# A transformer trunk with 2-D attention and an RWKV-7 scan: attention heads issued in pairs, scan features without half-height products and without Pool's products

## The chip, the cores and the metric

The kernel runs on one core of a Trainium2 chip. The core has a matrix engine (TensorE: PE, and PEld for its weight loads), a vector engine (DVE), a scalar engine (ACT), Pool (GpSimd) and a sync engine (SP) that mostly issues DMAs; each works through its own instructions in order and waits on semaphores for the others. Matrix products write PSUM, which DVE and ACT copy out. The metric is device time in microseconds of one execution; less is better.

## The reference

Two layers over 1024 latent tokens (a grid of 16 rows by 64 columns) and 256 context tokens, width 1024, float32. Layer 0 mixes with window pooling and neighbourhood attention, layer 1 with RWKV-7 in both directions; each layer ends with a squared-ReLU MLP. The two parts that the change touches:

```python
def neighbourhood_attention(q, k, v, k_ctx, v_ctx, rpb):
    ...
        s_lat = jnp.einsum('bqhd,brkhd->bhqrk', q_row, k_band).astype(jnp.float32) * scale
        ...
        s_lat = jnp.where(col_ok[:, None, :], s_lat + bias, NEG_INF)
        s_ctx = jnp.einsum('bqhd,bchd->bhqc', q_row, k_ctx).astype(jnp.float32) * scale
        s = jnp.concatenate([s_lat.reshape(B, NA_HEADS, GRID_W, kr * GRID_W), s_ctx], axis=-1)
        p = jax.nn.softmax(s, axis=-1).astype(v.dtype)
        ...
def rwkv_features(h, mu, ...):
    ...
    v = heads(xv @ wv)
    kk = heads(k * k_k)
    kk = kk * lax.rsqrt(jnp.maximum(jnp.sum(kk * kk, axis=-1, keepdims=True), 1e-24))
    ...
    for d in range(2):
        w_raw = heads(w0[d] + jnp.tanh(xw @ w1[d]) @ w2[d])
        decay = jnp.exp(-jnp.exp(-jax.nn.softplus(-w_raw) - 0.5))
        a = jax.nn.sigmoid(heads(a0[d] + (xa @ a1[d]) @ a2[d]))
        k_d = kh * (1 + (a - 1) * k_a_h)
```

## The kernel before

Stages follow each other on one core: layer 0's mixer (`l0_mixer`: norms, values, then the attention from 158 to about 575 us, then its output products), the MLP, the projections of layer 1 (`l1_features`), the scan features (`l1_scan_features`, about 1941 to 2299 us), the scan over chunks of 64 tokens (`l1_scan`), its readout, the last MLP. Large products split each float32 operand into a high and a low part (`split`: ACT casts the high part, DVE subtracts) and take three products (`mm3`); small ones are plain float32, and PE runs two instructions for each.

*Attention.* A unit is one head and one block of 128 queries: 8 heads in four pairs `hp` with member `hh`, 8 latent blocks (`rb`, `cb`) and 2 context blocks each, 80 units, the two heads of a pair one after the other. The two heads of a pair lie in the two halves of the 128 partitions (`half[hh]`). A unit's `scores` (L714) multiplies q and k over the head's 64 features: `sc`, 128 queries by 256 context keys, and for latent blocks `sl`, by 384 neighbouring keys. DVE adds the bias and finds the maximum, ACT takes the exponential with the sum. `normalise` (L743) divides on DVE. `transposed` (L749) turns five blocks of 128 keys on PE in groups of three and two (tile `ptps`), ACT and DVE copy them out. `outputs` (L766) multiplies by the values into 64 of the 128 partitions of `o`. The order is written out by hand: turn i issues scores of unit i, a fill, the transposes of unit i - 1, a fill, the outputs of unit i - 2, a fill, the normalising of unit i. A `fill` (L682) takes 1.17 steps of a generator `bg`, each one round of three products: first the projections of later heads and of the pooling (tile `acc`), then, when enough heads are done (`FIRST_OUT`, counted in units), the mixer's output products. What the fills haven't issued follows after the loop. PSUM: two buffers for `sl`, one for `sc`, two for `ptps`.

*Scan features.* A unit is 256 tokens by one pair of heads: 8 units of context tokens, then 32 of latent ones. In turn u:

- `decays(u+2)` multiplies the two lora inputs `xa` (decay and a, two directions d) by `w2h` over 128 rows (64 features twice: the inputs' high part in one half, their low part in the other) and by `w2l` over the 64 rows of the high part (tile `pw`, 8 products); ACT takes tanh of them (`sg`, `th`).
- `exps(u+1)` takes ACT's two exponentials of the running sums (`pe`, `cum`) and the key factor `kd`, which Pool multiplies by k.
- `scaled(u)` makes the four scaled features `F` on DVE; Pool copies the chunk ends to `pcs` and forms the bonus sums `ks`; SP writes `F` to DRAM.
- `scores(u-1)` takes the products `lp`, `bonuses(u-2)` multiplies `ks` (`bp`), `norms(u+2)` spreads the key norms by a product of 64 rows (`kn`, from `rn` and `sel`), `sums(u+2)` scans `sg` on DVE.
- Between them stand the value products (24 `acc` products over 128 rows, their transposes `vtr`). `value_lo` makes the low part `wl` of the next value weights, on Pool, once in four units. Steps of the first inversion (`tmp`, `X` on DVE) run along the latent units.

The scan's `chain_s` multiplies its state by a column of `pcs`.

Of the kernel before, what the change touches and what calls it, by code (L numbers as in the profile page):

```python
# [10 lines left out]
F32 = mybir.dt.float32  # L11
# [8 lines left out]
D = 1024  # L20
# [23 lines left out]
FIRST_OUT = 67  # L44
# [13 lines left out]
class Trunk:  # L58
# [240 lines left out]
    def l0_mixer(self):  # L299
# [143 lines left out]
        scp = self.pool(es, "scps", 1, PSUM)  # L443
        ptp = self.pool(es, "ptps", 2, PSUM)
# [106 lines left out]
        def out_products():  # L551
# [94 lines left out]
            for t in range(NT):  # L646
                ready = (FIRST_OUT, FIRST_OUT + 8, FIRST_OUT + 12)[(t + 1) // 4 if t + 1 < NT else 2]
# [53 lines left out]

        units = []
        for hp in range(4):
            units += [(hp, rb, cb, hh) for rb in range(2) for cb in range(4) for hh in range(2)]
            units += [(hp, None, t, hh) for t in range(2) for hh in range(2)]
        U = [dict() for _ in units]

        def bias_load(i):
            hp, rb, cb, hh = units[i]
            if rb is not None:  # L710
                b = U[i]["bias"] = atp.tile([128, 384], F32, tag="bias", name="bias", bufs=6)
                nc.sync.dma_start(out=b, in_=a["bias"][hp * 2 + hh, :, rb, CB_TYPE[cb]])

        def scores(i):  # L714
            hp, rb, cb, hh = units[i]
            w = U[i]
            q, k = qk[0, hp][half[hh]], qk[1, hp][half[hh]]
            if rb is None:
                q = q[:, L + cb * 128:L + (cb + 1) * 128]
            else:  # L720
                q = q[:, 0:L].rearrange("p (rb cb i) -> p rb cb i", rb=2, cb=4)[:, rb, cb]
            nl = 0 if rb is None else 384
            n = w["n"] = nl + 256
            sc = scp.tile([128, 256], F32, tag="sc", name="sc")
            nc.tensor.matmul(out=sc, lhsT=q, rhs=k[:, L:T], start=True, stop=True)
            p = w["p"] = atp.tile([128, 640], F32, tag="p", name="p", bufs=3)
            m = w["m"] = atp.tile([128, 8], F32, tag="m", name="m", bufs=3)
            nc.vector.tensor_tensor_reduce(
                out=p[:, nl:n], in0=sc, in1=zeros.to_broadcast([128, 256]), scale=1.0, scalar=-3.0e38, op0=ALU.add, op1=ALU.max, accum_out=m[:, 0:1]
            )  # L730
            top = m[:, 0:1]
            if nl:
                sl = slp.tile([128, 384], F32, tag="sl", name="sl")
                k3 = k[:, 0:L].rearrange("p (r c) -> p r c", c=GW)[:, 4 * rb:4 * rb + 12, C0[cb]:C0[cb] + 32]
                nc.tensor.matmul(out=sl, lhsT=q, rhs=k3, start=True, stop=True)
                nc.vector.tensor_tensor_reduce(
                    out=p[:, 0:nl], in0=sl, in1=w["bias"], scale=1.0, scalar=top, op0=ALU.add, op1=ALU.max, accum_out=m[:, 1:2]
                )
                top = m[:, 1:2]
            nc.vector.tensor_scalar(out=m[:, 2:3], in0=top, scalar1=-1.0, scalar2=None, op0=ALU.mult)  # L740
            nc.scalar.activation(out=p[:, 0:n], in_=p[:, 0:n], func=AF.Exp, bias=m[:, 2:3], accum_out=m[:, 4:5])  # L741

        def normalise(i):  # L743
            w = U[i]
            p, m, n = w["p"], w["m"], w["n"]
            nc.vector.reciprocal(out=m[:, 5:6], in_=m[:, 4:5])
            nc.vector.tensor_scalar(out=p[:, :n], in0=p[:, :n], scalar1=m[:, 5:6], scalar2=None, op0=ALU.mult)

        def transposed(i):  # L749
# [1450 lines left out]
```

## Time and profile before

| | us |
|---|---|
| median of 3 runs | 3671.38 (3670.8 to 3674.52) |
| profiled execution | 3669.7, its span 3667.9 |
| window 158 to 575 (attention) | 417 |
| window 1941 to 2299 (scan features) | 358 |

The profile is of one execution. PE's busy time is modelled, since matmuls overlap: the start of one to the start of the next says more than its duration. A group's row reads: line, engine, operation, output from inputs, shapes, count, then busy us and mean ns of one, then idle us before it and what ended that. In PE rows 64\*128 stands for 64 rows of the array by 128 columns. A row of a line's own view has minimum/median/maximum ns and the first and last start.

### The profile page before, as it was taken

The numbers are of one execution on the slowest core, as the hardware profiler recorded it, in microseconds if no ns is written. First come the engines' busy times: TensorE is split into PE (matmuls) and PEld (weight loads), VectorE is DVE, ScalarE is ACT, GpSimd is POOL, SyncE is SP. The second block draws the span as 40 slices with busy tenths as digits, with TensorE's granted clock in tenths as the row PEclk, the third lists the DMA queues.
The fourth block names the chain that finished last, engine by engine and source line by source line (L and its number), as shares of the span: only waits on it lengthen the run. The fifth ranks groups of instructions, "written<-read, shape, count | busy, mean of one in ns | idle before, by whom it ended". The sixth has DMA issues, their size and how long they took to land. (4 is left out here: it accounts for less than half of the span.)

```text
span 3667.9 us, 61460 instructions
## 1 busy us (share of the span) xinstructions
PE 3472.9 (95%) x25002; PEld 2833.8 (77%) x25002; DVE 2100.3 (57%) x3796; ACT 1445.7 (39%) x2659; POOL 583.4 (16%) x761
## 2 busy tenths in 40 slices
PE   8999999999999999999999998788988899999998
PEld 4777767788888888977887776677877688888887
DVE  4144555534444444477757989688755834444446
ACT  5223335522121211247767555656655441112122
POOL 0010020010101000004433555222231300000000
PEclk9999999999999999999998988799999999999999
DMA  8412224322222220133225666989885331111112
GB/s 278 139 58 69 62 91 132 130 84 80 92 70 92 69 74 31 58 111 94 82 79 156 202 213 207 207 179 196 186 200 146 130 101 46 46 46 47 52 52 75
DMA packets 434027, 409.05 MB, mean 112 GB/s; under 512 B 152992, under 2 KB 363808, under 8 KB 433744
## 3 DMA queue, kind: packets, MB, share of 16 engines
q1 hardware_dynamic: 405376, 321.55, 30.1%
q0 software_dynamic: 24032, 81.81, 8.1%
q8 instruction: 197, 3.23, 0.4%
q10 hardware_dynamic: 4336, 1.77, 0.2%
q14 instruction: 86, 0.70, 0.1%
HBM read 292.54 MB, written 112.49 MB: 110 GB/s over the span
## 5 line engine op out<-in xcount | busy, mean ns | idle before, releaser
L896 DVE TENSOR_TENSOR yacc<-yps,yacc 128x512 f32<-128x512 f32 x540 | 369.9, 690 | 304.1 <-PE yps L92 303.6
L73 ACT CAST wh<-st 128x1024 fp32r<-128x1024 f32 x160 | 165.1, 1048 | 758.2 <-PE yps L92 557.8
L92 PE MATMUL yps<-wh,xh 128*128 128x512 f32 x1152 | 453.2, 393 | 4.3 <-DVE yacc L896 2.6
L92 PE MATMUL yps<-wh,xl 128*128 128x512 f32 x1152 | 448.5, 390 | 1.4 <-DVE xl L74 1.4
L92 PE MATMUL yps<-wl,xh 128*128 128x512 f32 x1152 | 448.9, 390 | 0.0
L74 DVE TENSOR_TENSOR wl<-st,wh 128x1024 fp32r<-128x1024 f32 x160 | 194.4, 1229 | 264.8 <-ACT wh L73 262.6
L92 PE MATMUL acc<-h2h,wh 128*128 128x426 f32 (+3 forms) x768 | 274.4, 357 | 3.0 <-ACT y L670 3.0
L92 PE MATMUL acc<-h2h,wl 128*128 128x426 f32 (+3 forms) x768 | 273.2, 356 | 0.0
L92 PE MATMUL acc<-h2l,wh 128*128 128x426 f32 (+3 forms) x768 | 272.9, 355 | 0.0
L92 PEld LDWEIGHTS yps<-wh,xh 128*128 128x128 f32 x1152 | 216.2, 188 | 72.2 <-DVE yacc L896 13.2
L92 PEld LDWEIGHTS yps<-wh,xl 128*128 128x128 f32 x1152 | 216.2, 188 | 48.4 <-DVE xl L74 3.0
L92 PEld LDWEIGHTS yps<-wl,xh 128*128 128x128 f32 x1152 | 216.4, 188 | 44.9 <-issue 1.7
L878 DVE TENSOR_TENSOR r<-r 128x428 f32<-128x428 f32 (+4 forms) x164 | 102.4, 625 | 240.5 <-ACT r L877 240.5
L92 PE MATMUL acc<-mh,wh 128*128 128x256 f32 (+1 forms) x640 | 223.1, 350 | 4.3 <-ACT mh L73 4.2
L92 PE MATMUL acc<-ml,wh 128*128 128x256 f32 (+1 forms) x640 | 214.4, 335 | 0.0
L92 PE MATMUL acc<-mh,wl 128*128 128x256 f32 (+1 forms) x640 | 214.0, 335 | 0.0
L92 PE MATMUL acc<-h2bh,wh 128*128 128x512 f32 (+3 forms) x544 | 211.4, 389 | 1.4 <-ACT wh L73 0.7
L92 PE MATMUL acc<-h2bl,wh 128*128 128x512 f32 (+3 forms) x544 | 211.1, 388 | 0.8 <-DVE h2bl L287 0.7
L92 PE MATMUL acc<-h2bh,wl 128*128 128x512 f32 (+3 forms) x544 | 210.9, 388 | 0.3 <-DVE wl L74 0.3
L877 ACT ACTIVATE r<-acc 128x428 f32<-128x428 f32 (+4 forms) x164 | 89.1, 543 | 291.5 <-PE acc L92 272.5
L741 ACT ACTIVATE p<-p,m 128x640 f32<-128x640 f32 (+1 forms) x80 | 61.3, 766 | 260.2 <-DVE m L740 256.8
L92 PEld LDWEIGHTS acc<-h2h,wh 128*128 128x128 f32 x768 | 144.2, 188 | 15.9 <-issue 5.1
(324 smaller groups left out, 7520.7 us busy)
## 6 DMA issues: line engine op xcount, KB each, us to landing
st<-in_mlp_w SPq DMA_DIRECT2D x128, 512.0 KB
ft<-F SPq DMA_DIRECT2D x64, 512.0 KB
adas<-in_ada_w POOLq DMA_DIRECT2D x112, 256.0 KB, 3.8
adas<-in_ada_w SPq DMA_DIRECT2D x80, 256.0 KB
BK<-ft POOLq DMA_DIRECT2D x38, 512.0 KB, 6.9
AR<-ft POOLq DMA_DIRECT2D x64, 256.0 KB, 8.0
x<-x SPq DMA_DIRECT2D x28, 512.0 KB
bias<-in_bias SPq DMA_DIRECT2D x64, 192.0 KB
```

The costliest lines, as they stand in the source:

```text
L73: self.nc.scalar.copy(out=hi, in_=src)
L74: self.nc.vector.tensor_tensor(out=lo, in0=src, in1=hi.bitcast(F32), op=ALU.subtract)
L92: self.nc.tensor.matmul(out=ps, lhsT=lhs[x], rhs=rhs[y], start=first and i == 0, stop=last and i == 2)
L741: nc.scalar.activation(out=p[:, 0:n], in_=p[:, 0:n], func=AF.Exp, bias=m[:, 2:3], accum_out=m[:, 4:5])
L877: nc.scalar.activation(out=r, in_=ps, func=AF.Relu)
L878: nc.vector.tensor_tensor(out=r, in0=r, in1=r, op=ALU.mult)
L896: nc.vector.tensor_tensor(out=yacc[t][:, n], in0=ps, in1=yacc[t][:, n], op=ALU.add)
```

## The change

**Attention.** A unit is now a pair of heads, 40 units in all. `scores` issues the two heads' `sc` next to each other, then the two `sl`; DVE and ACT follow with both heads. `outputs` takes the two heads by turns for each block of keys. `transposed` treats the ten blocks of a pair (four in a context unit) in groups of four, four and two, called with a part number between the three fills. The outputs of unit i - 2 now stand right behind the scores of unit i. `sc` gets a second PSUM buffer, `ptps` loses one; `fill` takes 2.34 steps, and `FIRST_OUT` and the clocks count in pairs.

**Scan features.** `w2l`, `sel` and `rn` are 128 rows high, so the products `pw` and `kn` run over all rows; `w2l` then also meets the low part of its inputs. Pool's products (`kd`, `ks`, `value_lo`, half of the split of `w2l`) are made by DVE, and its copies to `pcs` by one copy on ACT; Pool keeps a small memset. `pcs` is laid out by pair and time block, and `chain_s` indexes it so. ACT's tanh is issued after `scaled` (`gates`), ACT's key factor behind it (`keys`); `bonuses` follows one unit behind. `v`, `ls`, `kd` and `ks` have one buffer in place of two, `th` two in place of three.

```diff
-FIRST_OUT = 67
+FIRST_OUT = 33
+FILL = 2.34
...
-        scp = self.pool(es, "scps", 1, PSUM)
-        ptp = self.pool(es, "ptps", 2, PSUM)
+        scp = self.pool(es, "scps", 2, PSUM)
+        ptp = self.pool(es, "ptps", 1, PSUM)
...
-            for _ in range(int(turn[0] * 1.17) - int((turn[0] - 1) * 1.17)):
+            for _ in range(int(turn[0] * FILL) - int((turn[0] - 1) * FILL)):
...
+            sc = [scp.tile([128, 256], F32, tag="sc", name="sc") for _ in two]
+            for hh in two:
+                nc.tensor.matmul(out=sc[hh], lhsT=qs[hh], rhs=ks[hh][:, L:T], start=True, stop=True)
             if nl:
-                sl = slp.tile([128, 384], F32, tag="sl", name="sl")
-                k3 = k[:, 0:L].rearrange("p (r c) -> p r c", c=GW)[:, 4 * rb:4 * rb + 12, C0[cb]:C0[cb] + 32]
-                nc.tensor.matmul(out=sl, lhsT=q, rhs=k3, start=True, stop=True)
...
+        def transposed(i, part):
+
             w = U[i]
-            p, n = w["p"], w["n"]
-            pt = w["pt"] = atp.tile([128, 640], F32, tag="pt", name="pt", bufs=2)
-            done = 0
-            for cnt in ((3, 2) if n == 640 else (2,)):
-                ps = ptp.tile([128, 384], F32, tag="pt", name="ptps")
-                for j in range(cnt):
-                    nc.tensor.transpose(
-                        out=ps[:, j * 128:(j + 1) * 128], in_=p[:, (done + j) * 128:(done + j + 1) * 128], identity=self.ident
-                    )
-                dst = pt[:, done * 128:(done + cnt) * 128]
-                if cnt == 3:
-                    nc.scalar.copy(out=dst, in_=ps[:, :cnt * 128])
-                else:
-                    nc.vector.tensor_copy(out=dst, in_=ps[:, :cnt * 128])
-                done += cnt
+            nb = w["n"] // 128
+            if part == 0:
+                w["pt"] = atp.tile([128, 2 * nb, 128], F32, tag="pt", name="pt", bufs=2)
+            blocks = [(hh, j) for hh in two for j in range(nb)][4 * part:4 * part + 4]
+            if not blocks:
+                return
+            ps = ptp.tile([128, 4, 128], F32, tag="pt", name="ptps")[:, :len(blocks)]
+            for b, (hh, j) in enumerate(blocks):
+                nc.tensor.transpose(out=ps[:, b], in_=w["p"][hh][:, j * 128:(j + 1) * 128], identity=self.ident)
+            dst = w["pt"][:, 4 * part:4 * part + len(blocks)]
+            if part == 1:
+                nc.vector.tensor_copy(out=dst, in_=ps)
+            else:
+                nc.scalar.copy(out=dst, in_=ps)
...
             for j, v in enumerate(vs):
-                nc.tensor.matmul(
-                    out=op[half[hh], cb], lhsT=v, rhs=w["pt"][:, j * 128:(j + 1) * 128], start=j == 0, stop=j == len(vs) - 1
-                )
+                for hh in two:
+                    nc.tensor.matmul(
+                        out=op[half[hh], cb], lhsT=v[:, half[hh]], rhs=w["pt"][:, hh * nb + j], start=j == 0, stop=j == nb - 1
+                    )
...
+                clock[0] = 2 * i
+                if i + 2 < nu:
+                    bias_load(i + 2)
+                if i % 10 == 2 and i < 30:
+                    heads(i // 10 + 1)
                 if i < nu:
                     scores(i)
+                if i > 1:
+                    outputs(i - 2)
                 fill()
                 if 0 < i <= nu:
-                    transposed(i - 1)
+                    transposed(i - 1, 0)
+                settle(2 * i)
                 fill()
-                if i > 1:
-                    outputs(i - 2)
-                settle(i)
+                if 0 < i <= nu:
+                    transposed(i - 1, 1)
+                clock[0] = 2 * i + 1
+                settle(2 * i + 1)
                 fill()
+                if 0 < i <= nu:
+                    transposed(i - 1, 2)
                 if i < nu:
                     normalise(i)
             settle()
...
-            wl = cp.tile([128, 2, D], F32R, name="w2l")
+            wl = cp.tile([128, 4, D], F32R, name="w2l")
             for i in range(4):
                 fr = slice(i * 256, i * 256 + 256)
                 wst = self.wst.tile([128, 4, 256], F32, tag="st", name="w2")
                 nc.sync.dma_start(out=wst, in_=a["w2s"][:, :, fr])
-                nc.scalar.copy(out=wh[:, :, fr], in_=wst)
-                for d in range(2):
-                    h = half[d]
-                    (nc.gpsimd if d else nc.vector).tensor_tensor(
-                        out=wl[h, :, fr], in0=wst[h, d::2], in1=wh[h, d::2, fr].bitcast(F32), op=ALU.subtract
-                    )
+                self.split(wh[:, :, fr], wl[:, :, fr], wst)
...
-        sel = cp.tile([64, 8, 128], F32R, name="sel")
+        sel = cp.tile([128, 8, 128], F32R, name="sel")
...
-            self.rn = bigp.tile([64, T], F32R, name="rn")
+            self.rn = bigp.tile([128, T], F32R, name="rn")
...
-                nc.gpsimd.tensor_tensor(out=vw[m + 1][1], in0=vst[0], in1=vw[m + 1][0].bitcast(F32), op=ALU.subtract)
+                nc.vector.tensor_tensor(out=vw[m + 1][1], in0=vst[0], in1=vw[m + 1][0].bitcast(F32), op=ALU.subtract)
...
-                    nc.tensor.matmul(out=ps[:, i], lhsT=wl[half[d], i, fr], rhs=x[half[d]], start=False, stop=True)
+                    nc.tensor.matmul(out=ps[:, i], lhsT=wl[:, 2 * i + d, fr], rhs=x, start=False, stop=True)
...
-            for d in range(2):
-                nc.gpsimd.tensor_tensor(out=kd[:, d], in0=kd[:, d], in1=rv(w["x"][:, 0], d), op=ALU.mult)
...
+            for d in range(2):
+                nc.vector.tensor_tensor(out=kd[:, d], in0=kd[:, d], in1=rv(w["x"][:, 0], d), op=ALU.mult)
...
+            nc.scalar.copy(out=self.pcs[:, hp, t0 // 256], in_=pe[:, :, CH])
...
-                nc.gpsimd.tensor_copy(out=self.pcs[:, d, hp, sl], in_=pe[:, cs, CH])
...
-                ks = w["ks"] = tp.tile([128, n], F32, tag="ks", name="ks", bufs=2)
-                nc.gpsimd.tensor_tensor(out=ks, in0=kd[:, 0], in1=rv(kd[:, 1], 1), op=ALU.add)
-                nc.gpsimd.tensor_tensor(out=ks, in0=ks, in1=rt, op=ALU.mult)
+                ks = w["ks"] = tp.tile([128, n], F32, tag="ks", name="ks", bufs=1)
+                nc.vector.tensor_tensor(out=ks, in0=kd[:, 0], in1=rv(kd[:, 1], 1), op=ALU.add)
+                nc.vector.tensor_tensor(out=ks, in0=ks, in1=rt, op=ALU.mult)
...
+                if u + 2 < nu:
+                    gates(u + 2)
+                if u + 1 < nu:
+                    keys(u + 1)
                 if u % 8 == 5 and u + 3 < nu:
                     self.xan = activations(self.xt)
                 if u + 3 < nu:
...
                     value_out(v - 1)
                 if u:
                     scores(u - 1)
-                if u >= 2:
-                    bonuses(u - 2)
+                    bonuses(u - 1)
...
-            for u in range(nu - 1, nu):
-                bonuses(u)
...
+                c = chunk_of(s, d)
+                pc = (c // 4) * 8 + d * 4 + (3 - c % 4 if d else c % 4)
                 nc.vector.tensor_tensor(
-                    out=SS[d], in0=src, in1=self.pcs[:, d, :, s:s + 1].to_broadcast([128, 8, CH]), op=ALU.mult
+                    out=SS[d], in0=src, in1=self.pcs[:, :, pc // 8, pc % 8:pc % 8 + 1].to_broadcast([128, 8, CH]), op=ALU.mult
                 )
```

PE near the end of the attention, where few products of other work stand between (`sc`, `sl` scores; `ptps` transposes; `o` outputs; `acc` a pooling product). Before, one unit and the next:

```order
L725 MATMUL sc<-kT,qT 128x256
L735 MATMUL sl<-kT,qT 128x384
L757 MATMUL ptps<-ident,p 128x128 x5
L781 MATMUL o<-pt,vlat 64x128 x3
L781 MATMUL o<-pt,vctx 64x128 x2
L496 MATMUL acc<-pd,poolw 128x426
L725 MATMUL sc<-kT,qT 128x256
```

And of the change, one pair:

```order
L731 MATMUL sc<-kT,qT 128x256 x2
L736 MATMUL sl<-kT,qT 128x384 x2
L795 MATMUL o<-pt,vlat 64x128 x6
L795 MATMUL o<-pt,vctx 64x128 x4
L772 MATMUL ptps<-ident,p 128x128 x4
L497 MATMUL acc<-pd,poolw 128x426
L772 MATMUL ptps<-ident,p 128x128 x4
L497 MATMUL acc<-pd,poolw 128x426
L772 MATMUL ptps<-ident,p 128x128 x2
```

Both heads' scores now stand together, the outputs come straight after them, and the transposes are parted by the fills.

DVE in one latent unit of the scan features (`th`, `F`: scaled features; `xa`: the next inputs' low part, only in one unit of eight; `cum`: the scan). Before:

```order
L1333 SCALAR_TENSOR_TENSOR th<-th,kk 128x256 x2
L1336 TENSOR_TENSOR F<-th,cum 128x8x64
L1340 TENSOR_TENSOR F<-kk,pe 128x4x64
L1342 TENSOR_TENSOR F<-kd,cum 128x4x64
L1347 TENSOR_TENSOR F<-k,pe 128x4x64
L1340 TENSOR_TENSOR F<-kk,pe 128x4x64
L1342 TENSOR_TENSOR F<-kd,cum 128x4x64
L1347 TENSOR_TENSOR F<-k,pe 128x4x64
L1206 TENSOR_TENSOR xa<-xt,xa 64x512 x2
L1305 SCALAR_TENSOR_TENSOR cum<-smask,sg 128x512
```

And of the change:

```order
L1357 SCALAR_TENSOR_TENSOR th<-th,kk 128x256 x2
L1360 TENSOR_TENSOR F<-th,cum 128x8x64
L1364 TENSOR_TENSOR F<-kk,pe 128x4x64 x2
L1366 TENSOR_TENSOR kd<-kd,k 128x256 x2
L1370 TENSOR_TENSOR F<-kd,cum 128x4x64
L1375 TENSOR_TENSOR F<-k,pe 128x4x64
L1370 TENSOR_TENSOR F<-kd,cum 128x4x64
L1375 TENSOR_TENSOR F<-k,pe 128x4x64
L1388 TENSOR_TENSOR ks<-kd 128x256
L1389 TENSOR_TENSOR ks<-ks,k 128x256
L1221 TENSOR_TENSOR xa<-xt,xa 64x512 x2
L1327 SCALAR_TENSOR_TENSOR cum<-smask,sg 128x512
```

DVE's own rows stay, and Pool's four products of 256 columns stand among them.

More of the change, by code (lines that the diff above doesn't have):

```diff
@@ new lines, in scores @@
+            if nl:
+                sl = [slp.tile([128, 384], F32, tag="sl", name="sl") for _ in two]
+                for hh in two:
+                    k3 = ks[hh][:, 0:L].rearrange("p (r c) -> p r c", c=GW)[:, 4 * rb:4 * rb + 12, C0[cb]:C0[cb] + 32]
+                    nc.tensor.matmul(out=sl[hh], lhsT=qs[hh], rhs=k3, start=True, stop=True)
+            w["p"] = [atp.tile([128, 640], F32, tag="p", name="p", bufs=4) for _ in two]
+            w["m"] = [atp.tile([128, 8], F32, tag="m", name="m", bufs=4) for _ in two]
@@ L736, in scores @@
+            for p, m, s in zip(w["p"], w["m"], sc):
                 nc.vector.tensor_tensor_reduce(
[L737 removed]
+                    out=p[:, nl:n], in0=s, in1=zeros.to_broadcast([128, 256]), scale=1.0, scalar=-3.0e38, op0=ALU.add, op1=ALU.max, accum_out=m[:, 0:1]
                 )
[L739 to L740 removed]
@@ L741, in scores @@
-            nc.scalar.activation(out=p[:, 0:n], in_=p[:, 0:n], func=AF.Exp, bias=m[:, 2:3], accum_out=m[:, 4:5])
+            for hh in two:
+                p, m = w["p"][hh], w["m"][hh]
+                top = m[:, 0:1]
+                if nl:
+                    nc.vector.tensor_tensor_reduce(
+                        out=p[:, 0:nl], in0=sl[hh], in1=w["bias"][hh], scale=1.0, scalar=top, op0=ALU.add, op1=ALU.max, accum_out=m[:, 1:2]
+                    )
+                    top = m[:, 1:2]
+                nc.vector.tensor_scalar(out=m[:, 2:3], in0=top, scalar1=-1.0, scalar2=None, op0=ALU.mult)
+                nc.scalar.activation(out=p[:, 0:n], in_=p[:, 0:n], func=AF.Exp, bias=m[:, 2:3], accum_out=m[:, 4:5])
@@ L767, in outputs @@
         def outputs(i):
-            hp, rb, cb, hh = units[i]
+            hp, rb, cb = units[i]
             w = U[i]
             vlat, vctx = att[hp]
-            first, last = (cb, hh) == (0, 0), (cb, hh) == ((1, 1) if rb is None else (3, 1))
+            first, last = cb == 0, cb == (1 if rb is None else 3)
             if first:
@@ L776, in outputs @@
             op, cat = att["o"], att["cat"]
-            vs = [vctx[:, j, half[hh]] for j in range(2)]
+            nb = w["n"] // 128
+            vs = [vctx[:, j] for j in two]
             if rb is not None:
-                vs = [vlat[:, cb * 4 + rb + j, half[hh]] for j in range(3)] + vs
+                vs = [vlat[:, cb * 4 + rb + j] for j in range(3)] + vs
             for j, v in enumerate(vs):
-                nc.tensor.matmul(
-                    out=op[half[hh], cb], lhsT=v, rhs=w["pt"][:, j * 128:(j + 1) * 128], start=j == 0, stop=j == len(vs) - 1
-                )
+                for hh in two:
+                    nc.tensor.matmul(
+                        out=op[half[hh], cb], lhsT=v[:, half[hh]], rhs=w["pt"][:, hh * nb + j], start=j == 0, stop=j == nb - 1
+                    )
             if last:
@@ L799, in l0_mixer @@
         heads(0)
-        for i in range(4):
+        for i in range(2):
             bias_load(i)
```

71 lines of the change are left out of this document (36 added, 35 removed).

## The prediction, made before the changed kernel was run

> **What bounds the kernel now.** I read the page's busy shares first, then the windows of the two stages that the change touches, then the PE timeline inside each, and last the groups of DVE.
>
> ```profile
> PE 3472.9 (95%) x25002; PEld 2833.8 (77%) x25002; DVE 2100.3 (57%) x3796; ACT 1445.7 (39%) x2659; POOL 583.4 (16%) x761
> ```
>
> PE is busy for 95% of the span, so what counts is how long PE's own stream is, stage by stage. The windows below are the attention (158 to 575 us), the context units of the scan features (1941 to 2010) and their latent units (2010 to 2299). Columns: length, then busy PE, PEld, DVE, ACT, POOL, granted clock, DMA share.
>
> ```profile
> 158.00:575.00 417.00, 406.71 (x2109) 290.31 (x2110) 213.44 (x667) 132.86 (x291) 40.15 (x25) 0.99 0.26 78
> 1941.00:2010.00 69.00, 69.00 (x527) 52.75 (x527) 51.02 (x84) 52.09 (x108) 25.20 (x45) 0.88 0.53 162
> 2010.00:2299.00 289.00, 258.02 (x2222) 209.72 (x2223) 266.93 (x489) 165.04 (x346) 159.08 (x239) 0.88 0.69 209
> ```
>
> The attention is bound by PE (406.7 of 417 us, DVE at half). The context units are too (69.0 of 69.0). The latent units are not: there DVE has 267 of 289 us and PE 258. So a saving on PE counts in full in the first two windows, and hardly in the third; there only DVE's sum counts.
>
> **The change, part by part: attention.** One head's turn on PE, with the fill products (`acc`, three per round) between:
>
> ```profile
> 301.41 0.70 PE L725 MATMUL sc<-kT,qT 64*128 64x256 f32 x2
> 301.95 0.80 PE L735 MATMUL sl<-kT,qT 64*128 64x384 f32 x2
> 302.68 0.47 PE L92 MATMUL acc<-h1h,wh 128*128 128x428 f32 x1
> 302.99 0.36 PE L92 MATMUL acc<-h1l,wh 128*128 128x428 f32 x1
> 303.18 0.36 PE L92 MATMUL acc<-h1h,wl 128*128 128x428 f32 x1
> 303.38 0.71 PE L757 MATMUL ptps<-ident,p 128*128 128x128 f32 x5
> 303.84 0.44 PE L92 MATMUL acc<-h1h,wh 128*128 128x428 f32 x1
> 304.12 0.36 PE L92 MATMUL acc<-h1l,wh 128*128 128x428 f32 x1
> 304.31 0.35 PE L92 MATMUL acc<-h1h,wl 128*128 128x428 f32 x1
> 304.59 0.87 PE L781 MATMUL o<-pt,vlat 128*64 128x128 f32 x6
> 305.30 0.60 PE L781 MATMUL o<-pt,vctx 128*64 128x128 f32 x4
> 305.83 0.46 PE L92 MATMUL acc<-h1h,wh 128*128 128x428 f32 x1
> ```
>
> Durations overlap, so I take differences of starts. Scores use 64 of 128 rows (64*128) and take 302.68 - 301.41 = 1.27 us; outputs use 64 of 128 columns (128*64) and take 305.83 - 304.59 = 1.24; five transposes take 0.46. A fill product normally steps by 0.19 (302.99 to 303.18), but by 0.31 right after the scores, 0.28 right after the transposes and 0.28 ahead of the outputs: each change of the array's shape costs some 0.1 us. A head has five such places (into and out of scores, into and out of outputs, out of the transposes), 0.5 us. A pair of heads thus costs 2 x (1.27 + 1.24 + 0.46 + 0.5) = 6.94 us beside its fill.
>
> What two heads cost when issued side by side in the two halves isn't shown in this stage, but the scan shows it:
>
> ```profile
> 2398.00 1.04 PE L1581 MATMUL sa<-AR,BK 128*64 128x128 f32 x16
> 2509.30 2.05 PE L1596 MATMUL sr<-AR,BK 128*128 128x128 f32 x16
> ```
>
> Both rows are 16 instructions over 128 columns; `sa` writes the two column halves by turns, `sr` uses the whole array. `sa` takes 1.04 us, `sr` 2.05: neighbours in different halves run at the same time. For outputs this is the very form (128*64, halves by turns), so a pair costs about 1.24 in place of 2.48. For row halves the nearest row is `lp` (quarters on the diagonal, rows and columns both different):
>
> ```profile
> 2099.78 1.15 PE L1370 MATMUL lp<-F 64*64 64x64 f32 x32
> 2100.86 0.61 PE L1385 MATMUL bp<-rkbd,ks 128*128 128x2 f32 x4
> 2101.40 0.38 PE L1298 MATMUL kn<-rn,sel 64*128 64x256 f32 x1
> 2101.71 0.38 PE L92 MATMUL acc<-mh,wh 128*128 128x256 f32 x1
> 2101.93 0.28 PE L92 MATMUL acc<-ml,wh 128*128 128x256 f32 x1
> 2102.05 0.28 PE L92 MATMUL acc<-mh,wl 128*128 128x256 f32 x1
> ...
> 2103.24 0.28 PE L1285 MATMUL pw<-xa,w2h 128*128 128x256 f32 x1
> 2103.45 0.38 PE L1286 MATMUL pw<-xa,w2l 64*128 64x256 f32 x1
> ...
> 2105.64 0.39 PE L92 MATMUL acc<-mh,wh 128*128 128x256 f32 x1
> ```
>
> 32 instructions of 64 columns in 1.08 us (2100.86 - 2099.78) are 2048 columns, as many as `sr`'s 16 of 128 in 2.05: again about half. So bounds for a pair's scores are 1.27 (full overlap) and 2.54 (none); I take 1.27, both overlapping rows being near a half. The Trainium skill ("TensorE: Matmul & The Clock Gate", Measured speedup vs the span model) gives four row tiles a speedup of 3.07, not 4. Two tiles at that efficiency would gain 1.54, and by an estimate from that page the attention would save about 13 us less than I say. No run here shows row halves alone.
>
> After the change a pair costs 1.27 + 1.24 + 0.92 for ten transposes, plus five places of 0.1 (into scores, out of outputs, out of three groups of transposes; scores and outputs now stand next to each other): 3.93 us. It saves 3.0 us for each of the 32 latent pairs. The 8 context pairs have 256 of 640 score columns (0.54 from 301.41 to 301.95) and 4 of 10 output products (0.53 from 305.30 to 305.83), so they save 0.54 + 0.53 + 0.5 = 1.6. Sum 32 x 3.0 + 8 x 1.6 = 109 us. Fill work is the same: 2.34 rounds for a pair against 1.17 for a head, thresholds halved.
>
> Costed at nothing: the second transpose buffer goes, so each group of four blocks must be copied out before the next. Between groups stands a fill of two or three rounds (2 x 0.58 = 1.2 us), which covers a copy of 512 columns (under 0.83, the exponential of 640 columns, quoted below). Near the end, where fills have no products left, the cover is gone and a copy costs up to 0.8 us three times for some five pairs. I take 4 us for that, so **attention -105**. After it DVE would have 213 of 312 us, 68%: still no bound.
>
> **Scan features, PE.** A 64-row product between 128-row ones costs 0.3 us in place of 0.12 (2101.93 to 2102.05): the eight `pw` products take 2105.64 - 2103.24 = 2.40 us, and over 128 rows 8 x 0.12 = 0.96. `kn` falls from 0.31 to 0.12 and its follower from 0.22 to 0.12. Together 1.7 us a unit. Over the nine units in the context window this is 15 us of 69, but ACT (52 us, plus small copies of `pcs`) and DVE (51, plus two products a unit for `kd`) are close behind. Bounds 3 and 15; I take 10.
>
> **Scan features, DVE.** In the latent window:
>
> ```profile
> L1340 DVE TENSOR_TENSOR F<-kk,pe 128x256 f32<-128x256 f32 x63 | 44.9, 712 | 0.0
> L1342 DVE TENSOR_TENSOR F<-kd,cum 128x256 f32<-128x256 f32 x64 | 37.8, 590 | 0.0
> L1333 DVE SCALAR_TENSOR_TENSOR th<-th,kk 128x256 f32<-128x256 f32 x62 | 32.2, 560 | 0.0
> L1347 DVE TENSOR_TENSOR F<-k,pe 128x256 f32<-128x256 f32 x64 | 31.9, 498 | 0.0
> L1323 POOL TENSOR_TENSOR kd<-kd,k 128x256 f32<-128x256 f32 x62 | 57.3, 942 | 87.3 <-ACT kd L1321 87.3
> L1232 POOL TENSOR_TENSOR wl<-st,wh 128x1024 fp32r<-128x1024 f32 x5 | 12.5, 2510 | 0.0
> L1347 DVE TENSOR_TENSOR F<-k,pe x64: 409/414/2556, 2010.1 to 2298.5; 128x256 f32<-128x256 f32 x64
> ```
>
> The last row gives minimum, median and maximum: the same product takes 409 ns or up to 2556, about the length of Pool's `wl`. I read the surplus as waiting for Pool's products. In the four groups it is (712 - 409) x 63 + (590 - 409) x 64 + (560 - 409) x 62 + (498 - 409) x 64 = 46 us. The change takes Pool's products away and gives DVE 62 for `kd`, 64 for `ks` and 5 for `wl`. Each of the first is at most 0.41; I take 0.35, since neighbours overlap a little, and 1.6 for `wl` (four times the width of 0.41): 44 + 8 = 52. So DVE has 267 - 46 + 52 = 273, and some 15 less for the surplus in its other groups, an estimate at a third of the four shown: 258 (bounds 250, and 319 if no surplus goes). Of its 22 idle us I leave 10: 268 in place of 289, **-21**.
>
> Two waits are added. With one `ks` buffer DVE's sum for a unit waits for PE's `bp` of the unit before, and behind it stand the scan, `kk` and the inversion. In the 31 units of the window PE needs 258/31 - 1.7 = 6.6 us each against DVE's 258/31 = 8.3, so `bp` comes first: nothing; without that lead, PE's 1.7 a unit would be lost. With one `kd` buffer ACT's `kd` waits for DVE's `ks`, and behind it stand the two copies out of PSUM, which PE awaits a unit later: nothing while ACT has slack (165 of 289). The wider split of `w2l` adds some 1 us on DVE ahead of the stage. **Features -30**.
>
> The sum against the profiled execution (3669.7 us, span 3667.9; the median of the runs shown is 1.7 us above): 3669.7 - 105 - 30 = **3535 us**.
>
> **Rivals.**
> Row halves don't overlap: scores stay at 2.54 a pair, 32 x 1.27 + 8 x 0.54 = 45 us come back, 3580. For it: no row shows 64*128 pairs. Against: `lp`. The Trainium skill ("TensorEngine Tiling (Array Packing)", Gotcha 1: PSUM Pressure) says that different row tiles cannot access the same PSUM bank at a time. By that rule this would happen if the two `sc` tiles shared a bank; the change gives that pool a second buffer, and no run here shows how it is placed. 13%.
>
> The surplus on DVE isn't Pool's: DVE then has 319 + 10 = 329 in place of 268, and the time is 3596. Against: the maxima lie at Pool's own length. 8%.
>
> The change doesn't do what it says: instructions don't overlap in either half, only changes of shape are saved (about 1 us a pair, 35 in all), 3605. Against: `sa`. 4%.
>
> Slower: PE waits in each turn for that pair's own chain.
>
> ```profile
> L741 ACT ACTIVATE p<-p,m 128x640 f32<-128x640 f32 x64 | 53.1, 830 | 210.4 <-DVE m L740 210.4
> L747 DVE TENSOR_SCALAR p<-p,m 128x640 f32<-128x640 f32 x64 | 43.2, 675 | 2.3
> L736 DVE CUSTOM_DVE_ANT_0 p<-sl,bias,m 128x384 f32<-128x384 f32 x64 | 39.6, 618 | 13.1 <-PE sl L735 11.8
> L728 DVE CUSTOM_DVE_ANT_0 p<-sc,zeros 128x256 f32<-128x256 f32 x80 | 33.9, 424 | 114.0 <-PE sc L725 113.9
> ```
>
> Unhidden, a turn is 3.9 on PE, 4.1 of fill (7 rounds of 0.58), 2 x (0.42 + 0.62) for the maxima, 1.7 for the exponentials and 1.35 for the normalising: 13.1 against 417/40 = 10.4 now, 40 x 2.7 = 108 us, and 3669.7 + 108 - 30 = 3748. It decides from 11.2 us a turn on (40 x 0.75 = 30). Against: transposes work one pair behind the scores, outputs two, so maxima, exponentials and normalising (5.1 us) have a whole turn of 8 us for themselves. 3%.
>
> **How the numbers follow.** Forecast 71%, the rivals 13, 8, 4 and 3%, and 1% that both gains are lost in waits and the time stays. The range takes the bounds of the forecast (attention -109 to -90, features -45 to -15: 3516 to 3565), the first rival and a margin below: 3508 to 3588; outside lie most of the other rivals, some 20%. A difference under 0.2% can't be told from none here. Faster by more: 96%, within: 1%, slower: 3%.
>
> **What would show it.** Attention window about 312 us; a pair's scores, first to next instruction, 1.3 us, its outputs 1.25. Features: `pw` steps of 0.12, DVE products near 410 ns without long ones, DVE over 93% busy in a latent part of about 268. Wrong would be: scores at 2.5; PE idle before the transposes; `ks` waiting for `bp`; a lower granted clock in the features, as PE idles more there.

## The result and the profile after

The changed kernel takes 3563.23 us (median of 4 runs, 3554.81 to 3569.77) against 3671.09 us for the kernel before, measured beside it: a ratio of 0.9704, 95% interval 0.9682 to 0.9725, so 108 us less where 135 were forecast. The profiled run is the fastest, 3554.81 us with a span of 3552.9.

The busy shares of its page (same columns as before):

```profile
PE 3314.0 (93%) x25002; PEld 2771.8 (78%) x25002; DVE 2063.3 (58%) x3899; ACT 1457.7 (41%) x2707; POOL 404.1 (11%) x526
```

PE lost 159 us of busy time, but the span fell by 115: some of what was saved on PE is now idle PE. The table gives the length of each stage, worked out in each trace as the difference of the first or last starts that bound it (`yps`: the MLP's products; `acc<-rwoh`: the readout's).

| stage (from, to) | before | after | difference | forecast |
|---|---|---|---|---|
| attention (first `sc`, last `o`) | 423.2 | 330.1 | -93.1 | -105 |
| last `o` to first `yps` | 127.2 | 128.0 | +0.8 | 0 |
| first `yps` to first `pw` | 1232.6 | 1240.0 | +7.4 | +1 |
| first `pw` to first `cum` | 5.6 | 3.5 | -2.1 | with the next |
| context units (first to 11th `cum`) | 66.7 | 57.9 | -8.8 | -10 |
| latent units (11th `cum` to last `lp`) | 285.9 | 270.9 | -15.0 | -21 |
| scan (last `lp` to first `acc<-rwoh`) | 500.9 | 496.0 | -4.9 | 0 |
| behind the scan (from `acc<-rwoh` on) | 868.0 | 868.0 | 0 | 0 |
| ahead of the attention | 157.9 | 158.5 | +0.6 | 0 |

**Attention.** PE's timeline for one pair in the steady part (start, duration; differences of starts are what counts):

```profile
422.87 0.70 PE L731 MATMUL sc<-kT,qT 64*128 64x256 f32 x4
423.41 0.81 PE L736 MATMUL sl<-kT,qT 64*128 64x384 f32 x4
424.15 0.88 PE L795 MATMUL o<-pt,vlat 128*64 128x128 f32 x12
424.86 0.61 PE L795 MATMUL o<-pt,vctx 128*64 128x128 f32 x8
425.39 0.46 PE L93 MATMUL acc<-h1h,wh 128*128 128x426 f32 x1
```

Both heads' scores take 424.15 - 422.87 = 1.28 us and both heads' outputs 1.24: a pair costs what one head cost. The windows of its steady part and of the stretch where the fill products have run out (columns as in the prediction's windows):

```profile
158.00:426.50 268.50, 264.31 (x1872) 214.59 (x1873) 153.25 (x537) 112.36 (x249) 22.39 (x18) 1.00 0.29 83
426.50:470.00 43.50, 26.79 (x161) 16.39 (x159) 32.03 (x66) 22.08 (x42) 16.74 (x7) 0.73 0.63 202
```

The loss is in the second row: PE is idle for 16.7 of 43.5 us there, and its granted clock is 0.73. What it waits for (waits of that window: total, times, longest):

```profile
PE ptps L772 <- ACT pt L777: 9.2, 3, 5.1
PE ptps L772 <- DVE pt L775: 3.7, 2, 2.9
PE ptps L772 <- DVE m L758: 2.8, 1, 2.8
```

These are the transposes with their one PSUM buffer. The next rows show why the copies and the normalising came so late, on DVE, Pool and ACT:

```profile
433.79 2.52 DVE L759 TENSOR_SCALAR p<-p,m 128x640 f32<-128x640 f32 x1
431.31 4.66 POOL L579 TENSOR_TENSOR wol<-st,woh 128x1024 fp32r<-128x1024 f32 x2 [1.38 <-ACT woh L576]
438.49 0.83 ACT L752 ACTIVATE p<-p,m 128x640 f32<-128x640 f32 x1 [5.53 <-DVE m L751]
440.12 1.97 ACT L576 CAST woh<-st 128x1024 fp32r<-128x1024 f32 x2
442.00 0.57 ACT L777 COPY pt<-ptps 128x512 f32<-128x512 f32 x1
```

A normalising product takes 2.52 us (0.56 elsewhere) while Pool splits the output weights `wol`, and ACT's copy out of the transposes stands behind the next pair's two exponentials, which waited 5.53 us for DVE's maximum, and behind two casts of `woh`.

**Features.** The windows of the context and the latent units:

```profile
1860.10:1918.00 57.90, 53.78 (x578) 50.32 (x578) 51.41 (x109) 52.06 (x118) 2.05 (x11) 0.92 0.67 201
1918.00:2189.00 271.00, 207.24 (x2165) 189.65 (x2163) 249.63 (x612) 167.38 (x371) 11.77 (x42) 0.88 0.75 222
```

DVE's groups in the latent window (busy, mean ns):

```profile
L1370 DVE TENSOR_TENSOR F<-kd,cum 128x256 f32<-128x256 f32 x62 | 26.0, 419 | 0.0
L1364 DVE TENSOR_TENSOR F<-kk,pe 128x256 f32<-128x256 f32 x62 | 23.4, 418 | 0.0
L1357 DVE SCALAR_TENSOR_TENSOR th<-th,kk 128x256 f32<-128x256 f32 x62 | 23.3, 418 | 0.0
```

These products, and `F<-k,pe` with 419, take 418 or 419 ns on average, where before the same groups stood at 498 to 712: the surplus is gone to the last. DVE works for 249.6 of 271.0 us, 92%; its longest waits there are these:

```profile
DVE tmp L1511 <- DMA M<-ls: 6.0, 1, 6.0
DVE tmp L1511 <- DMA xt<-ascr: 5.8, 1, 5.8
DVE ks L1388 <- PE bp L1413: 0.3, 1, 0.3
```

Two inversions wait for their loads (the second row names `xt`, whose loads stand behind `M`'s in the queue, though `tmp` reads only `M` and `X`); `ks` waits for `bp` for 0.3 us in all.

**Ahead of the features** (the row of +7.4), on PE and on SP's queue in the changed kernel:

```profile
1850.88 0.69 PE L1259 MATMUL vtr<-ident,vt 128*128 128x128 f32 x2 [8.32 <-ACT vt L1251]
1856.64 0.58 PE L1299 MATMUL pw<-xa,w2h 128*128 128x256 f32 x1 [5.07 <-DVE xa L1221]
...
1814.75 17.46 SPq L1141 DMA_DIRECT2D krs<-kt  x4
1841.88 2.09 SPq L1185 DMA_DIRECT2D w<-in_w2s  x2
1852.01 0.38 SPq L1262 DMA_DIRECT2D v1scr<-v  x1
1852.55 0.34 SPq L1213 DMA_DIRECT2D xt<-wscr  x1
```

PE waits 13.4 us. The last two loads of `w2` are issued behind the stores of the keys (`krs`), and the first load of `xt` behind the store of `v`. In the kernel before, both stood further ahead (the first `xt` at 1927.95 us, ahead of the store of `v` at 1939.70):

```profile
1894.92 1.63 SPq L1165 DMA_DIRECT2D w<-in_w2s  x2
1900.29 23.98 SPq L1121 DMA_DIRECT2D krs<-kt  x5
```

### The profile page after: what moved, and what is told of

The parts are those of the page before. It is cut to its first block, busy times and chain, and to the rows that moved or that the text cites. A ratio compares the mean times of both kernels' runs of the same rounds, so it can differ in the third digit from the quotient of the medians.

```text
span 3552.9 us, 61332 instructions
## 1 busy us (share of the span) xinstructions
PE 3314.0 (93%) x25002; PEld 2771.8 (78%) x25002; DVE 2063.3 (58%) x3899; ACT 1457.7 (41%) x2707; POOL 404.1 (11%) x526
## 5 line engine op out<-in xcount | busy, mean ns | idle before, releaser
L74 ACT CAST xh<-r 128x428 fp32r<-128x428 f32 (+4 forms) x164 | 93.3, 569 | 148.1 <-DVE r L898 148.1
```

The lines of the kernel that those rows point to most:

```text
L74: self.nc.scalar.copy(out=hi, in_=src)
```

## Experiments

Each whole-time ratio is against the kernel before, run beside it. Stage lengths are defined as in the table. `kd_pool`, `wol_dve`, `pt_acc`, `xt_first`, `sq_one` and `inv_later` were run once each and are read by stages. Runs whose edit leaves a stage of the changed kernel alone show how far it varies by itself: the attention 328.7 to 330.4 us, the stretch ahead of `pw` 1236.9 to 1240.0, the latent units 268.5 to 271.0.

**The two parts alone.** `attn_only` is the kernel before with the diff's pieces up to the attention's loop, `feat_only` with the pieces behind it.

> The kernel before with the attention's part of the change alone. Theory: the two parts act in stages that follow each other, so this one brings what the trace shows between the start of the attention and the MLP, 92 us: 3671 - 92 = 3579 us, and the features stay as they were (pw to the last lp 358 us). Rival: the parts help each other (the order of loads, the clock granted); then it brings under 85 or over 100 us.

> The kernel before with the features' part alone. Theory: -26 in the scan features, -5 in the scan, +7 at the boundary ahead of the features: 3671 - 24 = 3647 us, with the 13 us in which PE waits ahead of the first pw again. Rival: the boundary's 7 us come from the attention's shift of the stages in time; then 3640 us and no such wait.

Measured: 3594.45 us (0.9781, 0.9762 to 0.98) and 3657.35 us (0.9958, 0.9942 to 0.9975). By stages each part does just what it does in the changed kernel: the attention takes 330.0 us in the first (and 1231.9 us ahead of `pw`), and 423.4 in the second, whose stretch ahead of `pw` takes 1240.0, context units 58.0 and latent units 270.6. So +7.4 belongs to the features' part and not to a shift in time. The totals are each some 10 to 15 us above the theory. Against the kernel before beside it (3675.41 us) `attn_only` brings 81 us, which by the total alone is the rival's "under 85"; but its attention has the theory's length, and the loss stands in stages that it doesn't touch, with 510.6 us in the scan and 291.0 in the latent units. The profiled runs of all these kernels spread from 494.5 to 510.6 us in the scan. Its waits for loads differ most; here in the changed kernel (first row) and in `kd_pool`, below (second):

```profile
PE sa L1612 <- DMA AR<-ft: 4.8, 2, 2.8
...
PE sa L1612 <- DMA AR<-ft: 15.0, 4, 6.2
```

The change's -4.9 us in the scan is thus within what this stage varies by itself, and the median run's time fits a scan some 8 us longer than the profiled one's; the runs that weren't profiled don't show where they spent it.

**Do the halves overlap?** `out_by_head` issues a pair's outputs head after head:

```
-            for j, v in enumerate(vs):
-                for hh in two:
+            for hh in two:
+                for j, v in enumerate(vs):
```

> The changed kernel with the outputs of a pair issued head after head, five products in one column half and then five in the other, with as many changes of shape as before. Theory (neighbours in different halves run at the same time): the outputs' step goes from 1.24 to about 2.4 us a pair, 32 x 1.2 + 8 x 0.5 = +42 us, 3605 us. Rival (only the changes of shape were saved): the step stays at 1.25 and the time at 3563.

Measured: 3580.14 us (0.9744, 0.973 to 0.9759), the attention 345.5 us. Neither number came. PE's timeline of one pair's outputs shows why:

```profile
307.23 0.87 PE L795 MATMUL o<-pt,vlat 128*64 128x128 f32 x6
307.94 0.27 PE L795 MATMUL o<-pt,vctx 128*64 128x128 f32 x1
307.94 0.32 PE L795 MATMUL o<-pt,vlat 128*64 128x128 f32 x1
308.05 0.27 PE L795 MATMUL o<-pt,vctx 128*64 128x128 f32 x1
...
309.18 0.46 PE L93 MATMUL acc<-h1h,wh 128*128 128x428 f32 x1
```

The step is 309.18 - 307.23 = 1.95 us. The first six instructions run alone, 0.12 us each on average; the last four of the first head (`vctx`) then run beside the first of the second head (the `vlat` at 307.94), each half at its own pace. The halves do work at the same time, and the theory's only error was to take the order of issue for the order of start. Of the 32 x 0.71 = 23 us that the outputs grew, 15 show in the attention; PE's gaps over 0.3 us up to the last `o` shrank by some 3 us, the rest isn't accounted for.

**128 rows or 64 in the features?** `rows64` keeps Pool's products on DVE and puts the half-height products back:

```
-            wl = cp.tile([128, 4, D], F32R, name="w2l")
+            wl = cp.tile([128, 2, D], F32R, name="w2l")
...
-                    nc.tensor.matmul(out=ps[:, i], lhsT=wl[:, 2 * i + d, fr], rhs=x, start=False, stop=True)
+                    nc.tensor.matmul(out=ps[:, i], lhsT=wl[half[d], i, fr], rhs=x[half[d]], start=False, stop=True)
```

> The changed kernel with pw's second product and kn over 64 rows again (w2l, sel and rn of the old size); Pool's products stay on DVE. Theory: the context units are bound by PE and lose their 9 us; in the latent units DVE is the bound and PE's 1.7 us a unit hide, +0 to +10; the w2l tile of half the size is loaded and split early again, as in the kernel before, and the wait ahead of the first pw shrinks by 7 us: 3565 to 3575 us. Rival 1 (the rows bring the latent units' gain too): +15 or more there, 3580. Rival 2 (the wait ahead of pw has nothing to do with w2l's size): it stays at 13 us.

Measured: 3571.68 us (0.9723, 0.9704 to 0.9742): context units 65.8 us (+7.9), first `pw` to first `cum` 5.6 (+2.1), latent units 278.2 (+7.3), ahead of `pw` 1232.6 (-7.4). All four parts of the theory hold. DVE's busy time in the latent units is unchanged (250 us), and a new wait is there:

```profile
DVE ks L1391 <- PE bp L1416: 10.6, 6, 2.8
```

So the 128 rows bring 17 us in the features and cost 7 ahead of them. 7 of the 17 come by what the prediction named as the condition for one `ks` buffer: without PE's lead, `bp` comes last (10.6 us, while the waits for `M` shrink by 4.6).

**Is DVE's surplus Pool's work?** `kd_pool` gives the two `kd` products back to Pool, right behind ACT's key factor as in the kernel before; but ACT's key factor now stands behind `scaled`:

```
-            for d in range(2):
-                nc.vector.tensor_tensor(out=kd[:, d], in0=kd[:, d], in1=rv(w["x"][:, 0], d), op=ALU.mult)
...
+            for d in range(2):
+                nc.gpsimd.tensor_tensor(out=kd[:, d], in0=kd[:, d], in1=rv(w["x"][:, 0], d), op=ALU.mult)
```

> The changed kernel with kd's two products on Pool again. Theory (DVE stands still for a part of the time in which Pool works): the latent units of before had 68 us of surplus on DVE beside 157 us of Pool, 0.43 us for each; kd's 58 products of 0.94 us bring back 54 x 0.43 = 23 us of surplus and take 20 us of work off DVE, so the latent part stays near 271 us (268 to 278), with DVE products over 500 ns on average. Rival (only the long wl product was in the way): the latent part falls by 20 us to 251, and DVE's products keep their 419 ns.

One run, 3567.58 us; latent units 267.3 us, context units 59.7. The latent part came in just below the theory's range, and the averages over 500 ns did not come; the rival's 251 us is far off. Pool's and DVE's groups in its latent window:

```profile
L1349 POOL TENSOR_TENSOR kd<-kd,k 128x256 f32<-128x256 f32 x62 | 64.0, 1052 | 190.3 <-ACT kd L1347 190.3
L1366 DVE TENSOR_TENSOR F<-kk,pe 128x256 f32<-128x256 f32 x62 | 23.4, 418 | 0.0
L1359 DVE SCALAR_TENSOR_TENSOR th<-th,kk 128x256 f32<-128x256 f32 x62 | 25.2, 447 | 0.0
L1332 DVE SCALAR_TENSOR_TENSOR kk<-k,cols,kn 128x256 f32<-128x256 f32 x30 | 13.7, 456 | 0.8 <-DMA k<-krs 0.8
```

Of what stands beside `kd` in time, `th` goes from 418 to 447 ns, and the inversion's `tmp` and `X` from 0.34 to 0.41 and 0.45 us; `kk`, which reads the PSUM tile `kn`, starts while a `kd` product runs in 27 of its 30 turns and keeps the 456 ns that it takes in the changed kernel. The surplus adds up to some 15 us, 0.23 us for a us of Pool's and not 0.43, against some 21 us taken off DVE (62 products at a step of 0.34).

The trace of the kernel before says whose work the surplus there was. DVE's instructions that start while an operation of Pool runs exceed their undisturbed time by 27 us beside `kd`, by 27 beside `ks` and by 11 beside the five long `wl`, out of some 66 in all; beside the small copies to `pcs` none of 48 is longer. So Pool's products are the cause, and the rival's long product is a sixth of it. But `kd` could have stayed on Pool in its new place at no loss, and no run gives `ks` or `wl` back alone.

**The dry stretch of the attention.** `wol_dve` puts the splits of the output weights on DVE; `pt_acc` gives the transposes' second group a PSUM buffer of `acc` while no fill work needs it:

```
-                (nc.vector if k in (2, 5) else nc.gpsimd).tensor_tensor(
+                nc.vector.tensor_tensor(
```

```
+            if part == 1 and att.get("dry"):
+                ps = accp.tile([128, 512], F32, tag="acc", name="acc").rearrange("p (b f) -> p b f", f=128)[:, :len(blocks)]
+            else:
+                ps = ptp.tile([128, 4, 128], F32, tag="pt", name="ptps")[:, :len(blocks)]
```

> The changed kernel with all eight wol products (the lower halves of the output weights, loaded while the attention's fill work has run out) on DVE in place of two there and six on Pool. Theory: DVE's operations of 2.3 to 2.6 us beside them (a normalising product of 2.52 us in place of 0.56) go, and the transposes' waits with them: the attention falls from 330 to 325 us. Rival (the loads of the weights and ACT's casts set that stretch): 329 to 331.

> The changed kernel, where the second group of a pair's transposes goes to a PSUM buffer of acc while there is no fill work that needs it. Theory (one PSUM buffer for the transposes is what costs once the fill work has run out): the waits of 5.1, 3.6, 2.9 and 0.8 us before transposes shrink by 8 to 10 us in sum, the stretch at the lower clock behind them shortens, and the attention falls from 330 to 318 to 322 us. Rival (the pair's own chain takes their place): 327 to 330.

Attention 325.2 us with `wol` on DVE, as expected: the eight splits take 1.22 us each there and the normalising is back at 0.55 us. With the second buffer it is 327.1 us: the rival. Waits of PE in that stretch, with `wol` on DVE and, in the last two, with the buffer:

```profile
PE ptps L772 <- ACT pt L777: 10.0, 3, 5.8
PE ptps L772 <- DVE pt L775: 0.8, 1, 0.8
...
PE ptps L777 <- ACT pt L782: 6.0, 2, 3.2
PE ptps L777 <- DVE m L760: 2.8, 1, 2.8
```

Removing one wait leaves the next of the pair's own chain (exponential, normalising, copy), which has nothing beside it.

**The wait ahead of the features.** `xt_first` puts the loads of `xt` and `k` and the conversion of `xt` ahead of the value products' copies; `sq_one` frees 2 KB in each partition by one buffer fewer for the squares of the keys:

```
-        self.xt = load_act(L)
...
         with self.tc.manual_schedule():
+            self.xt = load_act(L)
```

```
-                    kt, sq = [ep.tile([128, 512], F32, tag=t, name=t)[:, :n] for t in ("kt", "sq")]
+                    kt, sq = [ep.tile([128, 512], F32, tag=t, name=t, bufs=b)[:, :n] for t, b in (("kt", 2), ("sq", 1))]
```

> The changed kernel with the first loads of xt and k ahead of the store of v in SP's queue, and the conversion of xt ahead of ACT's copy of the value products. Theory: the wait of 5.1 us ahead of the first pw goes; w2's late splits stay, so the stretch from the MLP to the first pw falls from 1240.0 to 1235 to 1237 us (before: 1232.6). Rival (xt's own data comes late): 1240.

> The changed kernel with one buffer in place of two for the squares of the keys (sq), which frees 2 KB in each partition of SBUF while w2 is loaded. Theory (w2l's doubled size did not fit beside the buffers of the key products, so that w2's loads and splits waited for those buffers): the loads go ahead again as in the kernel before, PE's waits of 13.4 us ahead of the first pw fall to about 6, and the stretch from the MLP to the first pw from 1240.0 to 1233 us. Rival (one sq buffer slows the key products as much, or the split itself is what is late): 1237 to 1241.

With `xt` first the stretch still takes 1239.0 us: the wait has only moved to the `vtr` ahead (first row below; ACT copies `vt` after the conversion now). With one `sq` buffer it takes 1232.7 us, and PE waits 6.8 us (last two rows); with the narrow `w2l` of `rows64` it is 6.5:

```profile
1855.41 0.69 PE L1259 MATMUL vtr<-ident,vt 128*128 128x128 f32 x2 [11.21 <-ACT vt L1251]
...
1848.05 0.69 PE L1259 MATMUL vtr<-ident,vt 128*128 128x128 f32 x2 [5.09 <-ACT vt L1251]
1850.43 0.58 PE L1299 MATMUL pw<-xa,w2h 128*128 128x256 f32 x1 [1.70 <-DVE xa L1221]
```

The last two loads of `w2` are issued 46 and 45 us ahead of the first `pw` in `sq_one`, as in the kernel before (46 and 45), and 15 and 13 us ahead of it in the changed kernel. The cause is space: `w2l` in double size did not fit beside the buffers of the key products, so its loads, casts and splits waited until those were free.

**The inversions' loads.** `inv_later` lets six steps in place of two pass between the request for `M` and its use:

```
-            for _ in range(2):
+            for _ in range(6):
                 yield
...
-                    for _ in range(int((u - 7) * 2.2) - int((u - 8) * 2.2)):
+                    for _ in range(int((u - 7) * 2.45) - int((u - 8) * 2.45)):
```

> The changed kernel with the first inversions started four steps (about two units) after their M is asked for, in place of two steps, and paced to end at the same unit. Theory (with DVE as the bound, its two idle stretches of 5.8 and 6.0 us, where a tmp product waits for the load of M, cost their whole length): both go, and the latent part falls from 270.9 to 259 to 261 us. Rival (another engine takes over as the bound): DVE idles elsewhere, 267 to 271.

The rival: latent units 269.8 us. DVE's timeline and the window of its new wait:

```profile
1940.08 0.48 DVE L1332 SCALAR_TENSOR_TENSOR kk<-k,cols,kn 128x256 f32<-128x256 f32 x1 [7.29 <-DMA k<-krs]
...
1932.00:1940.00 8.00, 1.31 (x11) 1.11 (x10) 0.79 (x1) 0.04 (x1) 0.00 (x0) 0.73 0.97 315
```

DVE now waits 7.3 us for `k`, while the DMA engines are busy to 97% with 315 GB/s. At the second inversion the wait for a load is gone, but DVE waits 1.4 and 1.8 us for PE there; its idle stretches over 0.3 us add up to 14.9 us, against 14.5. The queues are full, but not with `M` alone: between its eight loads (512 KB) and that of `k` SP issues the two of `xt`, the next value weights (512 KB) and two stores of `F` (512 KB each). No run tells their shares apart.

**Together.** `best` is `wol_dve`, `pt_acc`, `sq_one` and `inv_later` in one. `m_spread` leaves out `pt_acc` and asks for `M` in two fours:

```
+                    yield
+            X = ip.tile([128, 32, 32], F32, tag="X", name="X")
```

> The changed kernel with wol on DVE, a second PSUM buffer for the transposes while the fill work has run out, one sq buffer and the later inversions together. Theory: the parts add up: attention 330.1 to 320 (wol alone brought 5, the buffer alone 3, together some more since each left the other's wait standing), 1240.0 to 1233 ahead of pw, latent part 270.9 to 260: 28 us less, a median of 3535 us. Rival (the gains are not those of the places): over 3550.

> The changed kernel with wol on DVE, one sq buffer, and the eight loads of an inversion's M issued in two fours, one unit apart, in place of eight at once, with the inversion started some two units later. Theory (the eight loads of 128-byte rows fill the DMA queues for some 8 us, and whoever needs data behind them, M itself, k or the store of v, holds DVE up meanwhile; at half the size they fit beside the other transfers): DVE's idle stretches of 5 to 7 us in the latent part shrink to under 3 each and the latent part falls from 270.9 to 261 to 264 us; attention 325, 1232.6 ahead of pw; in sum 3563 - 5 - 7 - 8 = 3543 us. Rival (the transfers are the bound however they are laid): the idle stretches only move, the latent part stays at 267 to 271 and the time at 3550.

`best`: 3546.99 us (0.9643, 0.962 to 0.9667), attention 326.8, ahead of `pw` 1230.2, latent units 267.8. `m_spread`: 3541.19 us (0.9632, 0.9619 to 0.9645), with 325.4, 1231.3 and 267.0. Both beat the changed kernel. `best` misses its 3535 us: of its three places only the one ahead of `pw` came as expected, and the attention shows that the second buffer adds nothing to `wol_dve`. `m_spread` comes out near its 3543 us, but not for its reason: the latent units give 4 of the 8 us. The burst in halves did little: of DVE's waits for loads one of 4.8 us for `k` is left at 94% DMA, and two of 1.9 us for `M`. That `k` was asked for ahead of `M`'s second four, so a burst of eight can't be all that fills the queues. Most of the gain comes from the other two places.

```profile
DVE kk L1332 <- DMA k<-krs: 4.8, 1, 4.8
...
1918.00:1923.50 5.50, 1.17 (x10) 0.97 (x9) 0.73 (x2) 0.09 (x1) 0.00 (x0) 1.00 0.94 279
```

## Why the prediction was right, and where it missed

The forecast's mechanism held in each part, and 3563 us lies in the range; 27 us are missing from the 135. In the profiled run 20 of them stand in the table: 12 in the attention, 6 in the latent units and 6 ahead of the features, less 5 in the scan and small sums. The other 7 lie between that run and the median.

- **Scores and outputs of a pair**: 1.27 and 1.24 forecast, 1.28 and 1.24 measured. The rival of row halves that don't overlap is out, and so is the one of shape changes only (`out_by_head` puts 15 us back without adding a change of shape). That rival was also priced too high: by the prediction's own count a pair goes from ten changes of shape to five, 0.5 us, so 20 us in all and not 35. The Trainium skill's speedup of 3.07 for four row tiles ("TensorE: Matmul & The Clock Gate", Measured speedup vs the span model) would, by the prediction's estimate, have made two tiles gain 1.54; here two row halves gain the full factor of two (0.54 us for `sc` of one head before, 0.54 for two after).
- **The second transpose buffer, "costed" at 4 us**: this is the term that was mis-sized. The attention gave 93 and not 105 us. That is 16 us short of the 109 that the pairs were to bring. Gaps over 0.3 us on PE up to the last `o` add up to 19.9 us after and 10.0 before; some 3.5 more are an estimate for the half clock (below), at which PE is busy for 14.5 us of the attention after and 7.5 before. The rest stays open. The term was taken from the length of a copy (0.8 us); what the runs show is a queue: ACT's exponentials and casts ahead of the copy, and DVE's normalising held up by Pool's `wol`. The single buffer is one of several waits in a row, since `pt_acc` took back only 3 us and `wol_dve` 5. In this stretch the rival "PE waits for that pair's own chain" is true, for five turns of 40, and so is the sign of being wrong "PE idle before the transposes".
- **Context units**: -10 forecast, -10.9 with the step ahead of them. `rows64` puts it back, so it is PE's, as reasoned.
- **Latent units, DVE**: -21 forecast, -15.0 measured. The surplus went in full, in the other groups too, and DVE's busy time fell by 17 us and not by 9. But 10 us of idle time were assumed where 21 are: two waits of 5.8 and 6.0 us for the inversions' loads, which were already there before (5.0 and 4.2), and which `inv_later` and `m_spread` tie to full DMA queues. That term was a guess without a row. That two errors of 8 and 11 us nearly cancel is luck. The -15.0 is one run against one: `attn_only`, whose latent units are those of the kernel before, takes 291.0 us there, and against it the change brings 20.
- **One `ks` buffer, nothing**: right with 128 rows (0.3 us), and worth 10.6 us of waiting on DVE with 64. The two parts of the features' change need each other.
- **The wider `w2l`, +1**: it cost 7.4, PE's waits there going from 5.6 to 13.4 us. The price was taken from DVE's work; the size of the tile in SBUF was not weighed.
- **The scan**, nothing: its -4.9 us in the profiled run are not the change's, as far as the spread of this stage allows to say. In the profiled run they hide most of what the wider `w2l` cost beyond its forecast; that too is luck.
- **The clock in the features**: the feared lower clock did not come. The granted clock of the latent units is 0.88 before and after, though PE's busy time there fell from 258 to 207 us.

## What to carry to other kernels

When a change makes one engine's stream shorter, look for the places where its fill work ends: there every copy, cast and split in the other queues becomes its wait, and one buffer fewer no longer hides. Price a larger constant by the space it takes as well as by the work it adds: a tile that no longer fits beside its neighbours moves loads in another queue, far from the edit. An operation on Pool is not free because Pool is idle: weigh what DVE has to do at the same moment.

## What the runs showed of the hardware

- Two products in different column halves don't start in the order of issue: in `out_by_head` the second head's first product starts at 307.94 us, ahead of the first head's last three. About four instructions run ahead so: the context pairs' outputs, four and four, take 0.59 us in either order.
- A DVE instruction that reads only SBUF stands still for the rest of a two-input Pool product that it runs into: 2.52 us for a product of 0.56 beside a `wol` of 2.3. In the latent units before, of the 77 instructions for `F` that start while `kd`, `ks` or `wl` runs on Pool, 76 are held. The Trainium skill says that these two share ports by a lock that the first of them holds for the whole instruction, where DVE has two inputs in SBUF (or a two-port mode) and Pool reads SBUF ("SBUF — State Buffer", SBUF: two separate sides); the trace agrees for Pool's products, while beside its copies of four columns to `pcs`, which read SBUF too, none of 48 is held. `kk` with one input in PSUM is never held, in 27 meetings with `kd` in `kd_pool` and 12 with `ks` before, and products that don't meet Pool in time keep their 418 ns.
- From the end of a wait of 2.8 us on, through waits of 5.1 and 2.9 us, PE runs at half clock for some 17 us, and behind a wait of 3.6 us for some 7 again (granted clock, the third value from the end):

```profile
436.00:442.60 6.60, 1.09 (x4) 0.72 (x4) 5.10 (x16) 4.09 (x7) 0.43 (x1) 0.52 0.54 187
442.60:453.40 10.80, 7.84 (x36) 4.72 (x36) 9.48 (x19) 4.38 (x7) 4.36 (x2) 0.51 0.53 161
453.40:463.80 10.40, 6.30 (x48) 3.76 (x46) 6.78 (x16) 6.35 (x13) 4.92 (x2) 0.99 0.53 161
463.80:470.00 6.20, 5.33 (x31) 3.62 (x31) 4.05 (x12) 2.44 (x7) 0.00 (x0) 0.50 0.87 259
```

  The scores and outputs of the pair at 448.72 us take 4.7 us in place of 2.5, so a wait ahead of a bound engine costs more than its length.
